# A decoder trunk on one core: weights streamed in tiles of 2048 columns instead of 1024

## The chip, the cores and the metric

The kernel runs on one NeuronCore of a Trainium2 chip. The time is the device time of one execution in microseconds (us), the median of several runs. Engines are named as in the profile: PE (TensorE, matrix products), PEld (its weight loads), DVE (VectorE), ACT (ScalarE), POOL (GpSimd) and SP (SyncE, which only issues transfers here; SPq is its queue).

## The reference, cut to what matters

512 tokens of width 1024 pass two layers. Each layer is a mixer (layer 0: pooling and retention; layer 1: HGRN2), then PEER, a layer of 16384 experts of which each token picks 8 heads x 16; all in f32:

```python
def layer(h):
    mix = mixer(h)                              # projections of h, a recurrence, a projection out
    h = layer_norm(DN_ALPHA * h + mix)
    return layer_norm(DN_ALPHA * h + peer(h))

def peer(xt, w_q, sub_keys, u_tab, v_tab):      # 128 tokens at a time
    q = (xt @ w_q).reshape(T, 8, 2, 128)
    s = einsum('thpd,hpkd->thpk', q, sub_keys)
    s_top, i_top = top_k(s, 16)                 # per half of the key
    cand = s_top[:, :, 0, :, None] + s_top[:, :, 1, None, :]
    best, pos = top_k(cand.reshape(T, 8, 256), 16)
    eid  = the 16 expert numbers of each head at pos
    gate = softmax(best)
    act  = gelu(einsum('td,thkd->thk', xt, u_tab[eid]))
    return einsum('thk,thkd->td', gate * act, v_tab[eid])
```

## The kernel before

Every weight comes from HBM in f32, and PE multiplies in a shorter format. So each weight tile is split: `stream` takes a tile of 128 x 1024 from HBM (one transfer of 512 KB on SP's queue), ACT casts it to `hi` (L75) and DVE subtracts, `lo` = raw - hi (L76). Activations are split in the same way (`xThi`, `xTlo`). A product is three matmuls, hi x hi, hi x lo, lo x hi (`mm3`, L91 to L93). The tiles lie in rotating buffers: `raw` has 5 slots, `hi` and `lo` 6 each. A slot of `raw` is free when its `lo` is done, one of `hi` or `lo` when PE has read it last.

**Projections.** A weight matrix is handled in chunks of 512 columns, each of four tiles (two slices of 128 input channels in each). For each of the four blocks of 128 tokens PE makes 24 matmuls for a chunk: 8 slices by 3. After a mixer or a PEER the new activations are normalized, transposed on PE (L158) into PSUM tiles `pC`, of which there are three, and copied out by ACT (xThi, L163) and DVE (xTlo, L164).

**PEER.** Tokens 0 to 383 are computed densely: for each of 128 blocks of 128 experts, gelu(x u) is multiplied by a table of gates that is zero where a token did not choose an expert. The gate tables `gt` are built on PE from one-hot vectors (L785, L786), written to DRAM (`gd`) and loaded back by groups of four blocks, 768 KB each (L895). While DVE and ACT find the experts, `lookahead` computes gelu(x u) of the first 14 groups (`ge`). The last 128 tokens (`gather_rounds`) gather the rows of u and v of their own experts by indirect transfers that POOL issues (L838), into six row buffers; DVE multiplies (L848) and adds (L857) them.

**The expert loop** (L861 on) goes over the blocks: multiply `ge` by `gt` (L911), split the product into `ch` (ACT) and `cl` (DVE), stream the v tile (L915), and add hi x ch, lo x ch and hi x cl to the accumulators (`mm2`, L941; 18 matmuls of 512 columns for a block). From group 14 on `front` also streams u tiles and computes gelu(x u). A round of gathers is issued when a counter asks for it. The last four blocks are kept (`TAIL`) and finished one accumulator after another.

A scheduler in the tile framework fixes the order of the instructions on each engine when the kernel is built; an engine works strictly in that order, and an instruction that waits holds up all behind it.

## Time and profile before

| | us |
|---|---|
| median of 3 runs | 2877.6 (2876.41 to 2877.6) |
| the profiled execution | 2878.49 |
| its span, first to last instruction | 2876.7 |
| PE busy | 2859.1 (99%) |
| DVE busy | 2370.6 (82%) |
| ACT busy | 1144.2 (40%) |

The profile is of one execution. A row of a timeline has start and duration in us, then engine, line, operation, what is written<-what is read, shapes, and how many in a row; in brackets the idle time before it and what ended that. PE ran at the higher of its two clock levels all the time (mean granted clock 0.999).

### The profile page before, as it was taken

Reading aid. Unit: us, or ns where it says so; the run is one execution under the profiler, and the core shown is the slowest. Engines: PE = TensorE matmul, PEld = TensorE weight load, DVE = VectorE, ACT = ScalarE, POOL = GpSimd, SP = SyncE. Lnnn points to the kernel's source line nnn. Section 1 sums busy time; section 2 is a strip of 40 time slices with the busy share of each in tenths; the row PEclk is TensorE's granted clock in tenths of the full one; section 3 lists DMA queues with packets and bytes.
Section 4 is the critical chain, followed back from the end, with each engine's and each line's share of the span. In section 5 each row is a group of like instructions: output and inputs, shape, how many; then the busy total and the mean of one; then the engine's idle time right before and its main releaser. Section 6 shows DMA issues by size and latency. Waiting matters only on the chain.

```text
span 2876.7 us, 42571 instructions
## 1 busy us (share of the span) xinstructions
PE 2859.1 (99%) x15832; PEld 2556.6 (89%) x15832; DVE 2370.6 (82%) x4482; ACT 1144.2 (40%) x1707; POOL 721.3 (25%) x539
## 2 busy tenths in 40 slices
PE   9999999999999999999999999999999999999998
PEld 7888999988898888888888889999988989889887
DVE  6779999788878888886798679999788887888786
ACT  3333565433333333333334323565433333333332
POOL 0000000045445455440000000000245454544440
PEclk9999999999999999999999999999999999999999
DMA  6223469999999999995322234479999999989982
GB/s 223 94 94 111 147 208 289 273 366 376 350 339 370 341 376 334 351 359 169 107 81 70 96 96 134 152 244 291 313 375 343 353 370 336 375 332 352 352 323 74
DMA packets 283792, 743.41 MB, mean 258 GB/s; under 512 B 21696, under 2 KB 120512, under 8 KB 283584
## 3 DMA queue, kind: packets, MB, share of 16 engines
q1 hardware_dynamic: 209856, 472.22, 47.2%
q0 software_dynamic: 73728, 268.47, 24.1%
q8 instruction: 124, 2.03, 0.3%
q14 instruction: 84, 0.69, 0.1%
HBM read 669.31 MB, written 71.30 MB: 257 GB/s over the span
## 4 chain that ended last, share of the span: by engine, by line
PE 92%; DVE 5%; DMA 1%; ACT 1%; issue 1%; POOL 0%; SPq 0%; DVEq 0%; ACTq 0%
PE pB L941 18%; PE pC L941 18%; PE pA L91 14%; PE pA L93 14%; PE pA L92 14%; PE pC L91 2%; PE pC L93 2%; PE pC L92 2%; PE pB L785 1%; PE pB L786 1%; DVE lo L76 1%; DMA row<-in_u,eid 1%; DVE oh L778 1%; DVE og L779 1%; DVE s L701 1%
## 5 line engine op out<-in xcount | busy, mean ns | idle before, releaser
L75 ACT CAST hi<-raw 128x1024 fp32r<-128x1024 f32 (+1 forms) x609 | 638.1, 1051 | 662.1 <-PE pA L92 402.2
L76 DVE TENSOR_TENSOR lo<-raw,hi 128x1024 fp32r<-128x1024 f32 (+1 forms) x609 | 737.0, 1216 | 179.0 <-ACT hi L75 170.5
L838 POOL DMA_INDIRECT row<-in_u,eid x256 | 385.6, 1506 | 1493.7 <-DMA raw<-in_peer_v 884.7
L91 PE MATMUL pA<-xThi,hi 128*128 128x384 f32 (+2 forms) x2032 | 701.2, 345 | 3.7 <-ACT xThi L163 2.7
L93 PE MATMUL pA<-xThi,lo 128*128 128x384 f32 (+2 forms) x2032 | 699.3, 344 | 0.0
L92 PE MATMUL pA<-xTlo,hi 128*128 128x384 f32 (+2 forms) x2032 | 696.8, 343 | 0.6 <-DVE xTlo L76 0.6
L91 PEld LDWEIGHTS pA<-xThi,hi 128*128 128x128 f32 x2032 | 381.9, 188 | 21.5 <-ACT xThi L163 3.1
L92 PEld LDWEIGHTS pA<-xTlo,hi 128*128 128x128 f32 x2032 | 381.8, 188 | 17.8 <-DVE xTlo L76 1.3
L93 PEld LDWEIGHTS pA<-xThi,lo 128*128 128x128 f32 x2032 | 381.6, 188 | 14.4
L75 ACT CAST ch<-ge 128x384 fp32r<-128x384 f32 x256 | 131.4, 515 | 602.5 <-PE pC L941 473.3
L838 POOL DMA_INDIRECT row<-in_v,eid x256 | 328.7, 1284 | 158.4 <-DVE h L857 100.3
L857 DVE SCALAR_TENSOR_TENSOR h<-row,cf,h 128x1024 f32<-128x1024 f32 x256 | 327.8, 1280 | 1.1 <-DMA row<-in_v,eid 0.9
L848 DVE CUSTOM_DVE_ANT_0 row<-row,x 128x1024 f32<-128x1024 f32 x256 | 311.0, 1216 | 3.5 <-DMA row<-in_u,eid 3.5
L941 PE MATMUL pB<-hi,cl 128*128 128x512 f32 x768 | 299.4, 390 | 0.3 <-DVE cl L76 0.2
L941 PE MATMUL pC<-hi,ch 128*128 128x512 f32 x768 | 299.7, 390 | 0.0
L941 PE MATMUL pB<-lo,ch 128*128 128x512 f32 x768 | 299.6, 390 | 0.0
L941 PE MATMUL pC<-hi,cl 128*128 128x512 f32 x768 | 299.3, 390 | 0.0
L941 PE MATMUL pB<-hi,ch 128*128 128x512 f32 x768 | 298.8, 389 | 0.0
L941 PE MATMUL pC<-lo,ch 128*128 128x512 f32 x768 | 298.6, 389 | 0.0
L911 DVE TENSOR_TENSOR ge<-ge,gt 128x384 f32<-128x384 f32 x256 | 134.7, 552 | 160.4 <-DMA ge<-sp 144.6
L76 DVE TENSOR_TENSOR cl<-ge,ch 128x384 fp32r<-128x384 f32 x256 | 141.1, 552 | 62.0 <-ACT ch L75 61.4
L941 PEld LDWEIGHTS pB<-hi,cl 128*128 128x128 f32 x768 | 144.1, 188 | 32.5 <-DVE cl L76 1.3
(261 smaller groups left out, 4127.6 us busy)
## 6 DMA issues: line engine op xcount, KB each, us to landing
raw<-in_peer_ut SPq DMA_DIRECT2D x256, 512.0 KB
raw<-in_peer_v SPq DMA_DIRECT2D x256, 512.0 KB
gd<-gbuf SPq DMA_DIRECT2D x24, 2048.0 KB
gt<-gd SPq DMA_DIRECT2D x64, 768.0 KB
sp<-ge SPq DMA_DIRECT2D x24, 768.0 KB
ge<-sp SPq DMA_DIRECT2D x24, 768.0 KB
raw<-in_peer_w_q SPq DMA_DIRECT2D x32, 512.0 KB
raw<-in_c_w_in SPq DMA_DIRECT2D x32, 512.0 KB
```

Of the source, the lines that this page charges most:

```text
L75: self.nc.scalar.copy(hi, src)
L76: return self.nc.vector.tensor_tensor(lo, src, hi.bitcast(F32), ALU.subtract)
L91: nc.tensor.matmul(ps, ah, bh, start=(first and i == 0), stop=False)
L92: nc.tensor.matmul(ps, ah, bl, start=False, stop=False)
L93: nc.tensor.matmul(ps, al, bh, start=False, stop=(last and i == n - 1))
L701: nc.vector.match_replace(out=s2, in_to_replace=mx[:, 0:8], in_values=sc, imm_value=NEG)
L778: nc.vector.tensor_tensor(oh, iot[:, None, None].broadcast_to(b5), per(0), ALU.is_equal)
L838: nc.gpsimd.indirect_dma_start(out=t, out_offset=None, in_=io[name], in_offset=bass.IndirectOffsetOnAxis(ap=self.eid[:, j:j + 1], axis=0))
L848: nc.vector.tensor_tensor_reduce(ur, ur, x3, 1.0, 0.0, ALU.mult, ALU.add, av[:, k:k + 1])
L857: nc.vector.scalar_tensor_tensor(acc, vr, coefs[i // GQ][:, i % GQ:i % GQ + 1], acc, ALU.mult, ALU.add)
L911: nc.vector.tensor_tensor(gv, gv, gt[:, :, b, :], ALU.mult)
L941: nc.tensor.matmul(acc[hf], a[:, ts], b[:, hf * 512:(hf + 1) * 512], start=first and i == 0, stop=last and i == 2)
```

## The change

Tiles become 128 x 2048 (8 KB in each partition). One transfer of 1 MB, one cast and one subtraction now serve half a chunk of a projection, or two expert blocks. There are 3 slots each of `raw`, `hi` and `lo` instead of 5, 6 and 6. In the expert loop the multiplication by the gates and the split into `ch` and `cl` are also done for two blocks at once (128 x 768), and the rounds of gathers are issued per two blocks. Two small buffers share room with others to make space (`sg`, `sgc`). At the start of the kernel the transposed input and the first weights are loaded in parts of 1, 1, 2, 2 and 2 slices. The host lays the weights out accordingly. The diff, without the layouts and the renamings:

```diff
 NLA = 14
 KEEP = 2
 ROT = 3
-RAW = 5
+RAW = 3
+WIDE = 2048
 QS = 8
 Y2 = 1.4
 YC = (0.0, 0.0, 1.0, 4.0)
...
         E = ctx.enter_context
         self.const = E(tc.tile_pool(name="const", bufs=1))
         self.big = E(tc.tile_pool(name="big", bufs=1))
-        self.st = E(tc.tile_pool(name="st", bufs=6))
+        self.st = E(tc.tile_pool(name="st", bufs=3))
         self.raw = E(tc.tile_pool(name="raw", bufs=RAW))
         self.sm = E(tc.tile_pool(name="sm", bufs=4))
         self.dram = E(tc.tile_pool(name="dram", bufs=1, space=DRAM))
...
         self.nc.scalar.copy(hi, src)
         return self.nc.vector.tensor_tensor(lo, src, hi.bitcast(F32), ALU.subtract)
 
+    def wide(self):
+        return (self.raw.tile([P, WIDE], F32, name="raw", tag="raw"),
+                self.st.tile([P, WIDE], F32R, name="hi", tag="hi"),
+                self.st.tile([P, WIDE], F32R, name="lo", tag="lo"))
+
     def stream(self, src):
-        nc = self.nc
-        raw = self.raw.tile([P, 1024], F32, name="raw", tag="raw")
-        nc.sync.dma_start(out=raw, in_=src)
-        hi = self.st.tile([P, 1024], F32R, name="hi", tag="hi")
-        lo = self.st.tile([P, 1024], F32R, name="lo", tag="lo")
+        raw, hi, lo = self.wide()
+        self.nc.sync.dma_start(out=raw, in_=src)
         self.split(raw, hi, lo)
         return hi, lo
 
...
                 self.layernorm(tb, hs[tb], g, b, nxT, None if layer == 0 else out)
         return nxT
 
-    def mm1(self, layer, blk, xT, dst, alt=False):
-        nc = self.nc
-        uh, ul = self.stream(self.io["peer_ut"][layer, blk])
+    def mm1(self, u, b, xT, dst, alt=False):
         if alt:
             ps = self.psC.tile([P, 512], F32, name="pC", tag="pC")
         else:
             ps = self.psA.tile([P, 512], F32, name="pA", tag="pA")
-        self.mm3(ps[:, :TD], [((uh[:, dc * P:(dc + 1) * P], ul[:, dc * P:(dc + 1) * P]),
-                               (xT[0][:, dc, :TD], xT[1][:, dc, :TD])) for dc in range(NDC)])
-        nc.scalar.activation(dst, ps[:, :TD], AF.Gelu)
+        c = [slice((b * NDC + dc) * P, (b * NDC + dc + 1) * P) for dc in range(NDC)]
+        self.mm3(ps[:, :TD], [((u[0][:, c[dc]], u[1][:, c[dc]]), (xT[0][:, dc, :TD], xT[1][:, dc, :TD]))
+                              for dc in range(NDC)])
+        self.nc.scalar.activation(dst, ps[:, :TD], AF.Gelu)
 
     def lookahead(self, layer, xT, sp):
         for g in range(NLA):
             ge = self.pe.tile([P, NB, TD], F32, name="ge", tag="ge", bufs=3)
             for b in range(NB):
-                self.mm1(layer, g * NB + b, xT, ge[:, b, :], b % 2 == 1)
+                if b % 2 == 0:
+                    u = self.stream(self.io["peer_ut"][layer, (g * NB + b) // 2])
+                self.mm1(u, b % 2, xT, ge[:, b, :], b % 2 == 1)
                 if g >= NLA - KEEP:
                     self.kept[g] = ge
                 elif b == NB - 1:
...
                     nc.sync.dma_start(out=gt, in_=gd[g])
                     ges[g] = (ge, gt)
                 if g >= NLA:
-                    self.mm1(layer, g * NB + b, xT, ges[g][0][:, b, :])
-
-            for i in range(AHEAD):
+                    u = self.stream(io["peer_ut"][layer, (g * NB + b) // 2])
+                    for k in range(2):
+                        self.mm1(u, k, xT, ges[g][0][:, b + k, :])
+
+            for i in range(0, AHEAD, 2):
                 front(i)
-            cs, vs = [], []
-            for i in range(NE):
-                if i % 2 == 0:
-                    front(i + AHEAD)
-                    front(i + AHEAD + 1)
+            tail = []
+            for i in range(0, NE, 2):
+                front(i + AHEAD)
                 g, b = order[i // NB], i % NB
                 ge, gt = ges[g]
-                gf = ge[:, b, :]
-                gv = gf.rearrange("p (s t) -> p s t", t=32)
-                nc.vector.tensor_tensor(gv, gv, gt[:, :, b, :], ALU.mult)
-                ch = ex.tile([P, TD], F32R, name="ch", tag="ch", bufs=4)
-                cl = ex.tile([P, TD], F32R, name="cl", tag="cl", bufs=4)
+                gf = ge[:, b:b + 2, :]
+                gv = gf.rearrange("p b (s t) -> p b s t", t=32)
+                nc.vector.tensor_tensor(gv, gv, gt[:, :, b:b + 2, :].rearrange("p s b t -> p b s t"), ALU.mult)
+                ch = ex.tile([P, 2, TD], F32R, name="ch", tag="ch")
+                cl = ex.tile([P, 2, TD], F32R, name="cl", tag="cl")
                 mark = self.split(gf, ch, cl)
-                v = self.stream(io["peer_v"][layer, g * NB + b])
-                cs.append((ch, cl))
-                vs.append(v)
-                if i < NE - TAIL and i % 2:
-                    for k in (i - 1, i):
+                v = self.stream(io["peer_v"][layer, (g * NB + b) // 2])
+                for k in range(2):
+                    c = (ch[:, k], cl[:, k])
+                    vk = [x[:, k * D:(k + 1) * D] for x in v]
+                    if i < NE - TAIL:
                         for tb in range(3):
-                            self.mm2(accs[tb], tb, cs[k], vs[k], k == 0, False)
-                used += 1.0 if g < NLA else 2.0
+                            self.mm2(accs[tb], tb, c, vk, i + k == 0, False)
+                    else:
+                        tail.append((c, vk))
+                used += 2.0 if g < NLA else 4.0
                 while done < (P + 8) * used / (total * 0.96):
                     done += 1
                     with tc.issue_after(mark.ins):
...
             for tb in range(3):
                 for hf in range(2):
                     for b in range(TAIL):
-                        self.mm2(accs[tb], tb, cs[b - TAIL], vs[b - TAIL], False, b == TAIL - 1, (hf,))
+                        self.mm2(accs[tb], tb, *tail[b], False, b == TAIL - 1, (hf,))
                     z = hs[tb][:, hf * 512:(hf + 1) * 512]
                     nc.vector.scalar_tensor_tensor(z, z, ALPHA, accs[tb][hf], ALU.mult, ALU.add)
 
...
     def run(self, out):
         nc, io = self.nc, self.io
         self.epst = self.const.tile([P, 1], F32, name="epst", tag="epst")
-        self.const.tile([P, 344], F32, name="gap", tag="gap")
+        self.const.tile([P, 88], F32, name="gap", tag="gap")
         nc.vector.memset(self.epst, EPS)
         hs = [self.big.tile([P, D], F32, name="h%d" % tb, tag="h%d" % tb) for tb in range(NTB)]
         xT = self.new_xT()
         self.warm()
-        w0 = []
-        for k in range(4):
-            raw = self.raw.tile([P, 2, T], F32, name="raw", tag="raw")
-            if k == 0:
-                wr = self.raw.tile([P, 2, T], F32, name="raw", tag="raw")
-                hi = self.st.tile([P, 2, T], F32R, name="hi", tag="hi")
-                lo = self.st.tile([P, 2, T], F32R, name="lo", tag="lo")
-                wsrc = io["ab_w_in"][0, 0].rearrange("p (a n) -> p a n", a=2)
-                for a in range(2):
-                    nc.sync.dma_start(out=raw[:, a], in_=io["xT"][:, a, :])
-                    nc.sync.dma_start(out=wr[:, a], in_=wsrc[:, a])
-                for a in range(2):
-                    self.split(raw[:, a], xT[0][:, a, :], xT[1][:, a, :])
-                    self.split(wr[:, a], hi[:, a], lo[:, a])
-                flat = "p a n -> p (a n)"
-                w0.append((hi.rearrange(flat), lo.rearrange(flat)))
-                continue
-            ks = slice(2 * k, 2 * k + 2)
-            nc.sync.dma_start(out=raw, in_=io["xT"][:, ks, :])
-            self.split(raw, xT[0][:, ks, :], xT[1][:, ks, :])
-            w0.append(self.stream(io["ab_w_in"][0, k]))
+        self.w0 = []
+        for k, parts in ((0, ((0, 1), (1, 2), (2, 4))), (1, ((0, 2), (2, 4)))):
+            raw = self.raw.tile([P, 4, T], F32, name="raw", tag="raw")
+            wr, hi, lo = self.wide()
+            for a, b in parts:
+                nc.sync.dma_start(out=raw[:, a:b], in_=io["xT"][:, 4 * k + a:4 * k + b, :])
+                nc.sync.dma_start(out=wr[:, a * T:b * T], in_=io["ab_w_in"][0, k][:, a * T:b * T])
+            for a, b in parts:
+                d = slice(4 * k + a, 4 * k + b)
+                self.split(raw[:, a:b], xT[0][:, d], xT[1][:, d])
+                self.split(wr[:, a * T:b * T], hi[:, a * T:b * T], lo[:, a * T:b * T])
+            self.w0.append((hi, lo))
         self.ident = self.cload("ident", [P, P])
-        self.w0 = w0
         for layer in range(2):
             self.mixer(layer, xT, hs)
             xT = self.peer(layer, hs, out)
```

Three lines are added at the head of the file, so the lines after are a few higher: the cast is L76, the subtraction L77, `mm3` L94 to L96, the transposes L161, xThi L166, xTlo L167, the gates' multiplication L915, the u rows L852.

Where the order of instructions changes. The first place is the start of PEER in layer 0, on DVE. `h2` and `h3` are residuals of token blocks 2 and 3, the other names are as above; the number behind a name marks the single tile. Before the change:

```order
L171 RECIPROCAL rs_1355<-sd_1353 128x1
L76 TENSOR_TENSOR lo_1442<-raw_1439,hi_1441 128x1024
L194 SCALAR_TENSOR_TENSOR h2_86<-h2_86,rs_1355,lnb_1289 128x512 x2
L204 SCALAR_TENSOR_TENSOR h3_87<-h3_87,pA_1254 128x512
L76 TENSOR_TENSOR lo_1448<-raw_1445,hi_1447 128x1024
L164 TENSOR_TENSOR xTlo_1293<-pC_1306,xThi_1292 128x4x128
L164 TENSOR_TENSOR xTlo_1293<-pC_1314,xThi_1292 128x4x128
L164 TENSOR_TENSOR xTlo_1293<-pC_1333,xThi_1292 128x4x128
L164 TENSOR_TENSOR xTlo_1293<-pC_1341,xThi_1292 128x4x128
L186 BN_STATS bst_1375<-h3_87 128x6
L164 TENSOR_TENSOR xTlo_1293<-pC_1360,xThi_1292 128x4x128
L164 TENSOR_TENSOR xTlo_1293<-pC_1368,xThi_1292 128x4x128
```

The same piece after the change (L77 for L76, L167 for L164):

```order
L197 SCALAR_TENSOR_TENSOR h2_86<-h2_86,rs_1287,lnb_1221 128x512 x2
L77 TENSOR_TENSOR lo_1367<-raw_1365,hi_1366 128x2048
L207 SCALAR_TENSOR_TENSOR h3_87<-h3_87,pA_1186 128x512
L77 TENSOR_TENSOR lo_1703<-raw_1701,hi_1702 128x2048
L167 TENSOR_TENSOR xTlo_1225<-pC_1238,xThi_1224 128x4x128
L167 TENSOR_TENSOR xTlo_1225<-pC_1246,xThi_1224 128x4x128
L167 TENSOR_TENSOR xTlo_1225<-pC_1265,xThi_1224 128x4x128
L167 TENSOR_TENSOR xTlo_1225<-pC_1273,xThi_1224 128x4x128
L167 TENSOR_TENSOR xTlo_1225<-pC_1292,xThi_1224 128x4x128
L167 TENSOR_TENSOR xTlo_1225<-pC_1300,xThi_1224 128x4x128
```


The two narrow `lo` ahead of the first xTlo are two wide ones now, so twice as many columns are subtracted ahead of it; before, the next narrow ones came behind the sixth xTlo.

On ACT at the same place (sd is a standard deviation), before the change:

```order
L169 ACTIVATE sd_1326<-mv_1324,epst_81 128x1
L75 CAST hi_1441<-raw_1439 128x1024
L169 ACTIVATE sd_1353<-mv_1351,epst_81 128x1
L75 CAST hi_1447<-raw_1445 128x1024
L75 CAST hi_1783<-raw_1781 128x1024
L75 CAST hi_1789<-raw_1787 128x1024
L163 CAST xThi_1292<-pC_1306 128x4x128
L163 CAST xThi_1292<-pC_1314 128x4x128
L163 CAST xThi_1292<-pC_1333 128x4x128
L163 CAST xThi_1292<-pC_1341 128x4x128
```

After the change:

```order
L172 ACTIVATE sd_1285<-mv_1283,epst_81 128x1
L76 CAST hi_1366<-raw_1365 128x2048
L76 CAST hi_1702<-raw_1701 128x2048
L166 CAST xThi_1224<-pC_1238 128x4x128
L166 CAST xThi_1224<-pC_1246 128x4x128
L166 CAST xThi_1224<-pC_1265 128x4x128
```


Four narrow casts between the standard deviations and xThi have become two wide ones. hi_1360 and hi_1366 are the first two tiles of w_q, hi_1702 the third; with three slots hi_1366 takes the one of the first half of the last chunk of the mixer's output projection, and hi_1702 the one of its second half.

The second place is the passage from layer 0 to layer 1, on ACT. Before the change:

```order
L169 ACTIVATE sd_12997<-mv_12995,epst_81 128x1
L169 ACTIVATE sd_13024<-mv_13022,epst_81 128x1
L75 CAST hi_13119<-raw_13117 128x1024
L75 CAST hi_13125<-raw_13123 128x1024
L75 CAST hi_13235<-raw_13233 128x1024
L163 CAST xThi_12963<-pC_12977 128x4x128
L163 CAST xThi_12963<-pC_12985 128x4x128
L163 CAST xThi_12963<-pC_13004 128x4x128
L75 CAST hi_13241<-raw_13239 128x1024
L163 CAST xThi_12963<-pC_13012 128x4x128
```

After the change:

```order
L172 ACTIVATE sd_11793<-mv_11791,epst_81 128x1
L172 ACTIVATE sd_11820<-mv_11818,epst_81 128x1
L76 CAST hi_11908<-raw_11907 128x2048
L76 CAST hi_12018<-raw_12017 128x2048
L166 CAST xThi_11759<-pC_11773 128x4x128
L166 CAST xThi_11759<-pC_11781 128x4x128
L166 CAST xThi_11759<-pC_11800 128x4x128
```


Three narrow casts ahead of xThi are two wide ones, and the narrow one between the copies is gone. On DVE one wide `lo` (lo_11909) stands where one narrow one stood, ahead of the first xTlo.

The third place is the start of the expert loop in layer 0, on DVE. ge_5997 (before) and ge_5713 (after) are the group that is multiplied first, gt_5998 and gt_5714 its gate table; ge_5405 and ge_5145 the second group with the second table, gt_6128 and gt_5832. Before the change:

```order
L911 TENSOR_TENSOR ge_5997<-ge_5997,gt_5998 128x384 x2
L76 TENSOR_TENSOR lo_6275<-raw_6272,hi_6274 128x1024
L76 TENSOR_TENSOR cl_6132<-ge_5997,ch_6131 128x384
L848 ISA row_6142,av_6141<-row_6142,x3_1287 128x1024
L848 ISA av_6141 128x1
L848 ISA row_6145,av_6141<-row_6145,x3_1287 128x1024
L848 ISA av_6141 128x1
L76 TENSOR_TENSOR cl_6150<-ge_5997,ch_6149 128x384
L848 ISA row_6195,av_6141<-row_6195,x3_1287 128x1024
L848 ISA av_6141 128x1
L911 TENSOR_TENSOR ge_5997<-ge_5997,gt_5998 128x384 x2
L911 TENSOR_TENSOR ge_5405<-ge_5405,gt_6128 128x384
```

After the change:

```order
L915 TENSOR_TENSOR ge_5713<-ge_5713,gt_5714 128x768
L915 TENSOR_TENSOR ge_5145<-ge_5145,gt_5832 128x768
L77 TENSOR_TENSOR cl_5836<-ge_5713,ch_5835 128x768
L852 ISA row_5882,av_5881<-row_5882,x3_1219 128x1024
L852 ISA av_5881 128x1
L852 ISA row_5885,av_5881<-row_5885,x3_1219 128x1024
L852 ISA av_5881 128x1
L852 ISA row_5888,av_5881<-row_5888,x3_1219 128x1024
L852 ISA av_5881 128x1
L915 TENSOR_TENSOR ge_5713<-ge_5713,gt_5714 128x768
L77 TENSOR_TENSOR lo_5956<-raw_5954,hi_5955 128x2048
L77 TENSOR_TENSOR cl_5893<-ge_5713,ch_5892 128x768
```


Before, the first two `cl` and three rows of gathered tokens stood ahead of the multiplication by the second table (gt_6128); now the multiplication by the second table (gt_5832) is the second instruction of the piece, ahead of the first `cl`. In layer 1 the order is the same, with other numbers.

## Rows read from the trace of the kernel before

**Rows 1.** The page, part 1: busy us (share of the span) x instructions.

```profile
PE 2859.1 (99%) x15832; PEld 2556.6 (89%) x15832; DVE 2370.6 (82%) x4482; ACT 1144.2 (40%) x1707; POOL 721.3 (25%) x539
```

**Rows 2.** PE's waits: what waited <- for what: us in total, times, longest.

```profile
PE pA L91 <- ACT xThi L163: 2.9, 3, 1.3
...
PE pA L91 <- ACT hi L75: 1.0, 1, 1.0
```

**Rows 3.** ACT's groups by shape: count | busy, mean ns | idle before, releaser.

```profile
L75 ACT CAST hi<-raw 128x1024 fp32r<-128x1024 f32 x607 | 636.8, 1053 | 660.5 <-PE pA L92 402.2 <-issue 100.3 <-PE pC L92 78.2
L75 ACT CAST ch<-ge 128x384 fp32r<-128x384 f32 x256 | 131.4, 515 | 602.5 <-PE pC L941 473.3 <-DVE ge L911 102.9 <-issue 21.2
...
L75 ACT CAST hi<-raw 128x512 fp32r<-128x512 f32 x2 | 1.2, 618 | 1.6 <-DMA raw<-in_ab_w_in 1.6
```

**Rows 4.** DVE's groups by shape.

```profile
L76 DVE TENSOR_TENSOR lo<-raw,hi 128x1024 fp32r<-128x1024 f32 x607 | 735.6, 1218 | 177.9 <-ACT hi L75 169.5 <-PE pB L786 5.4
...
L76 DVE TENSOR_TENSOR cl<-ge,ch 128x384 fp32r<-128x384 f32 x256 | 141.1, 552 | 62.0 <-ACT ch L75 61.4
...
L76 DVE TENSOR_TENSOR lo<-raw,hi 128x512 fp32r<-128x512 f32 x2 | 1.4, 688 | 1.0 <-ACT hi L75 1.0
```

**Rows 5.** Line L75: ACT's idle time ahead of it (us, times) until this.

```profile
  DMA raw<-in_peer_ut: 18.4, 5
```

**Rows 6.** Timeline of the start of PEER in layer 0.

```profile
162.78 1.47 PE L158 MATMUL pC<-c_ident,h 128*128 128x128 f32 x12
...
163.68 1.22 DVE L76 TENSOR_TENSOR lo<-raw,hi 128x1024 fp32r<-128x1024 f32 x1
163.97 1.55 ACT L163 CAST xThi<-pC 128x512 fp32r<-128x512 f32 x3
164.81 1.88 DVE L164 TENSOR_TENSOR xTlo<-pC,xThi 128x512 fp32r<-128x512 f32 x3
...
165.58 0.39 PE L91 MATMUL pA<-xThi,hi 128*128 128x256 f32 x1 [1.33 <-ACT xThi L163]
...
167.39 0.36 PE L92 MATMUL pA<-xTlo,hi 128*128 128x256 f32 x1
```

**Rows 7.** The layer boundary: first a piece of the chain of waits, then timeline.

```profile
1366.75 2.72 PE pB L941 x12
...
1381.07 2.95 ACT L75 CAST hi<-raw 128x1024 fp32r<-128x1024 f32 x3 [1.19 <-PE pC L941]
...
1383.92 1.59 ACT L163 CAST xThi<-pC 128x512 fp32r<-128x512 f32 x3
...
1384.64 0.48 PE L91 MATMUL pA<-hi,xThi 128*128 128x512 f32 x1
```

**Rows 8.** The experts' start in layer 0: timeline; then transfers from 567 to 577.

```profile
566.54 0.80 SPq L895 DMA_DIRECT2D gt<-gd  x2
...
573.27 1.03 DVE L911 TENSOR_TENSOR ge<-ge,gt 128x384 f32<-128x384 f32 x2 [4.51 <-DMA gt<-gd]
...
574.74 0.39 PE L941 MATMUL pB<-hi,ch 128*128 128x512 f32 x1
...
575.35 0.55 DVE L76 TENSOR_TENSOR cl<-ge,ch 128x384 fp32r<-128x384 f32 x1
...
581.48 1.49 DVE L911 TENSOR_TENSOR ge<-ge,gt 128x384 f32<-128x384 f32 x3
...
DMA packets 872, 3.71 MB, mean 371 GB/s; under 512 B 95, under 2 KB 95, under 8 KB 872
...
q1 hardware_dynamic: 572, 2.59, 69.9%
```

**Rows 9.** Timeline of the experts' start in layer 1.

```profile
2058.16 1.03 DVE L911 TENSOR_TENSOR ge<-ge,gt 128x384 f32<-128x384 f32 x2 [4.18 <-DMA gt<-gd]
...
2059.96 0.39 PE L941 MATMUL pB<-hi,ch 128*128 128x512 f32 x1
```

**Rows 10.** The page, part 5: the rows of u on DVE.

```profile
L848 DVE CUSTOM_DVE_ANT_0 row<-row,x 128x1024 f32<-128x1024 f32 x256 | 311.0, 1216 | 3.5 <-DMA row<-in_u,eid 3.5
```

More of the change, by code (lines that the diff above doesn't have):

```diff
@@ L98, in wchunk @@
             return w
-        return [self.stream(src[j, k]) for k in range(4)]
+        return [self.stream(src[j, k]) for k in range(2)]
     def proj_T(self, src, j, xT, sink, early=False):
@@ L224, in mixer_ab @@
             sums = self.pool_part(ab, xT, ya, w, icnt, pw, psc)
-            self.w0 = [self.stream(w[1, k]) for k in range(4)]
+            self.w0 = [self.stream(w[1, k]) for k in range(2)]
             nc.sync.dma_start(out=ng, in_=io["ret_norm_g"][0][None, :].broadcast_to([P, 512]))
```

18 lines of the change are left out of this document (9 added, 9 removed).

## The prediction

> **What bounds the kernel now.** I read the busy shares first: TensorE works 2859.1 of 2876.7 us [rows 1], so nearly all of the time is its own work. The question is then what TensorE waits for. The view of its waits answers [rows 2]: the longest entry is 2.9 us for xThi, the high half of the transposed activations, and it waited for a weight tile's high half once, 1.0 us. All entries of that view add up to about 7 us. The other engines' busy time is therefore cover, not path: the change can give back at most these 7 us, while every place where a bigger step makes TensorE wait is paid in full, because nothing later has room to make it up. The profiled execution took 2878.5 us, 0.9 above the median of 2877.6; the sum is made on it, and the median taken by adding the same difference.
>
> TensorE's matmuls themselves don't change: the same products, shapes and nearly the same order. So the work is to find the places where a tile's own chain (transfer, cast on ScalarE, subtraction on VectorE) now finishes later than TensorE asks for it.
>
> **What a wide step costs.** A cast of 1024 columns takes 1.053 us and one of 512 takes 0.618 [rows 3]: 0.435 per 512 columns, so 2048 columns take 1.053 + 2 x 0.435 = 1.92 us (estimate). A subtraction takes 1.218 at 1024 and 0.688 at 512 [rows 4]: 1.218 + 2 x 0.530 = 2.28 us (estimate). The same slope puts a `cl` over two blocks (768 columns) at 0.552 + 0.40 = 0.95 us, the multiplication at the same (two narrow ones took 1.03 [rows 8]), and a `ch` at 0.515 + 0.33 = 0.84. Per pair of blocks VectorE saves about 0.15 us each on `lo`, `cl` and `ge`, and ScalarE 0.19 on the cast. Over some 300 pairs of tiles and 128 pairs of expert blocks this is over 80 us of VectorE's time, and I count it at nothing: among TensorE's waits the one for `hi` is 1.0 us [rows 2] and those for any low half are shorter. If that cover were gone the saving could be at most the 7 us above. What grows is the latency: from a free slot to a usable `lo` was 1.05 + 1.22 = 2.3 us, and is 4.2 us.
>
> What the transfers are worth can be bounded as well. ScalarE waited for a raw transfer of `peer_ut` 18.4 us in 5 places of the whole run [rows 5], TensorE not once. The Trainium skill (DMA: Bandwidth & Descriptors, "Rules for kernel authors") asks for 1 MiB per transfer for the most bandwidth, which speaks for this change; here the trace sets the worth of that against TensorE's waits and leaves next to nothing. Its best result is the rival "faster" below.
>
> **Start of PEER (both layers), +1.9 us each.** The last chunk of the mixer's output projection ends at 162.78 [rows 6]. Before, ScalarE casts two more w_q tiles and starts xThi at 163.97; TensorE waits 1.33 us for it. With three wide slots the second wide tile of the next chunk (hi_1366) takes the slot of the old chunk's first tile, free 12 matmuls before the end (12 take 2.72 [rows 7]), about 160.1; it is done by 162.1. The tile after it (hi_1702) needs the slot that is free at 162.8, runs 163.0 to 164.9, and stands ahead of xThi in ScalarE's row. xThi starts 0.95 late. On VectorE the two wide subtractions stand ahead of the first xTlo: lo_1367 162.15 to 164.4, the residual addition to 165.0, lo_1703 to about 167.3. Before, the second `lo` started at 163.68 and the first xTlo at 164.81 [rows 6]. The transposes that follow reuse the PSUM tile that each xTlo has read; the sixth waits for the third xTlo, which was done at 166.69 (164.81 + 1.88) and now is at 167.3 + 1.9 = 169.2. TensorE's first L92 then comes at about 169.3 instead of 167.39: +1.9. In layer 1 the same rows stand 1485 us later, so +3.8 in all. The bounds: +0.95 per layer, if only the cast matters, and +2.5, if the wide operations run 10% over the estimate: 1.9 to 5.
>
> **Layer boundary, +1.5 us.** The experts' last six groups of 12 matmuls begin at 1366.75 and end near 1382.9 [rows 7]; TensorE goes on with the next mixer's first L91 at 1384.64. The tail holds two tiles to its end. Before, three short casts ran from 1381.07 and xThi followed at 1383.92. Now hi_11908 gets the slot of the tail's first pair about 6 matmuls (1.4 us) before the end, 1381.6 to 1383.5, and hi_12018 that of the second pair, to 1385.4; xThi is behind both: 1385.4 against 1383.92, +1.5. VectorE's lo_11909 (to about 1386.5) delays xTlo by 1.3, which is no more. Bounds 0.9 to 2.
>
> **Start of the experts (both layers), +6.6 us.** This is the largest term. The two gate tables `gt` of the first two groups are requested at 566.54; the first lets VectorE multiply at 573.27 after 4.51 us of waiting; `cl` follows at 575.35 [rows 8]. The second table was wanted only by the third multiplication of the group that starts at 581.48. Now VectorE's row has the multiplication by the **second** table directly behind the first, ahead of the first `cl`. So `cl`, the rows of the gathered tokens and everything behind wait for the second load. When does it land? After 573.27 and before 582.42 (581.48 + two thirds of 1.49) by the rows. Between: the queue of these loads moved 69.9% of 371 GB/s there, 259 GB/s [rows 8]; 0.79 MB more takes 3.0 us, and 5.1 us if the 0.52 MB weight tile requested behind it gets its share at once. I take the middle, 577.3. Then the multiplication 0.95 and `cl` 0.95 end at 579.2, where TensorE, without waiting, would ask at 574.74 + 4 x 0.23 = 575.65: **3.5 us**. In layer 1 the first table is there at 2058.16 and the first matmul comes later, at 2059.96 [rows 9]: the second at 2062.1 by the same rates, `cl` at 2064.0, asked for at 2060.9: **3.1 us**. Nothing gives that back: the next pair's `cl` comes behind three rows of 1.3 us, another multiplication and a wide `lo`, about 8 us after the first, which is what 36 matmuls last (8.2 us), so the delay is passed on and not repeated. Bounds per layer: 0.4 us (the table lands with the first; only the wider `ch` counts) and 8.7 us (582.42 + 1.9 - 575.65): 0.8 to 17.4.
>
> **Everywhere else, 0.** *Inside the expert loop* TensorE reads a pair for 8.2 us (36 matmuls of 0.227) or more, against a chain of 4.2 us, and had no wait there. *Chunk changes:* the second wide tile of the next chunk has the window from 12 matmuls before the end of the old chunk to 12 after: 24 x 0.227 = 5.45 us for 4.2 us of work. It fits with 1.2 us to spare, and that is the rival below. *Start:* the first parts of xT and weights are as large as before; the later ones are together as large. 0, or up to 1 us late. *Gathers:* VectorE waited 3.5 us in all for u rows [rows 10]; issued in bursts of three rounds at most, they keep the same six buffers.
>
> **Sum.** 3.8 + 1.5 + 6.6 = 11.9 us: 2890.4 beside the profiled 2878.5, and from the median **2889.5 us**. The bounds of the three terms add up to 3.6 and 24.4, which gives 2881 to 2902 from the median.
>
> **The rivals.** *Same, about 2882 (chance 0.21):* the second gate table is there when the first is, since both are requested in one go and share 16 engines; then the experts' start costs 0.8, and with PEER's start at its lower bound of 1.9 and the boundary's 1.5 the sum is +4.2. For it: VectorE's wait of 4.51 us was ended by the first table alone, and no row shows the second's end. Against it: the queue's rate, by which the second needs at least 3 us more. The point is 575.3: a table that is usable by then costs little. *Faster, about 2871 (0.06):* the larger transfers and the fewer fixed parts remove the waits of 7 us and the three terms don't appear, because VectorE, relieved of 0.15 us per operation, reaches them earlier. Against it: freed slots and the landed table, not the engines, set the times there. *Much slower, about 2909 (0.11):* the chunk changes. There are some 20 of them in the projections; the window leaves 1.2 us, so one further operation of 0.7 us ahead of the wide tile fits in, two do not. If each is missed by 1 us, 20 are added to the 11.9. For it: VectorE is busy for most of the span [rows 1] and also does the lookup there; against it: in most chunk changes the wide cast stands ahead of the last copies out of PSUM in ScalarE's row. *The forecast* (0.62) is the rest.
>
> **How the numbers follow.** A measurement of this kernel tells about 0.2% (5.8 us) from no change: 2871.8 to 2883.4. Faster has the chance of its rival, 0.06. Same takes the rival of 0.21 and 0.04 of the forecast's low end: 0.25. Slower is the rest, 0.69. The range leaves out the faster rival and the much slower one (0.17 together). It goes from 2877, no change at all, since the bounds of the same case lie between that and 2884, to 2902, the upper bound of the sum.
>
> **What the profile after would show.** Right: TensorE waits for `cl` some 3 us once per layer at the experts' start, with VectorE's second multiplication waiting for gt<-gd just before; first low-half matmul of PEER about 6.5 us after the transposes begin, not 4.6; first matmul of the second mixer 3 us after the experts' end, not 1.7; TensorE's waits near 19 us in all. Wrong: a wait for `hi` or `lo` at many chunk changes (the slower rival), no wait for `cl` (the same), or VectorE waiting for u or v rows many times, which none of my terms holds. If the wide cast takes other than 1.9 us or the wide subtraction other than 2.3, the first two terms are wrong in size.

## The result, and the profile after

The changed kernel takes **2892.8 us** (median of 5 runs, 2889.0 to 2896.1) against 2877.6 (5 runs): ratio 1.0052, 95% interval 1.0038 to 1.0067. It is slower by 15 us, three from the forecast of 2889.5. The two times agree better than their parts do: the largest term never appeared, another was nearly twice as large, places held at nothing cost 9 us, and a gain was overlooked.

The page after, parts 1 and 5 (compare [rows 1], [rows 3], [rows 4]):

```profile
PE 2862.6 (99%) x15832; PEld 2558.5 (89%) x15832; DVE 2337.3 (81%) x3924; ACT 1086.3 (38%) x1277; POOL 844.0 (29%) x539
...
L77 DVE TENSOR_TENSOR lo<-raw,hi 128x2048 fp32r<-128x2048 f32 (+1 forms) x307 | 694.8, 2263 | 176.8 <-ACT hi L76 176.6
L76 ACT CAST hi<-raw 128x2048 fp32r<-128x2048 f32 (+1 forms) x307 | 580.5, 1893 | 419.5 <-PE pA L95 262.3
...
L76 ACT CAST ch<-ge 128x768 fp32r<-128x768 f32 x128 | 107.0, 836 | 614.3 <-PE pC L947 601.0
...
L77 DVE TENSOR_TENSOR cl<-ge,ch 128x768 fp32r<-128x768 f32 x128 | 122.3, 956 | 228.5 <-ACT ch L76 228.5
```

The wide steps cost what was estimated (the estimate in brackets): 1.89 us (1.92), 2.26 (2.28), 0.84 (0.84) and 0.96 (0.95). TensorE works 3.5 us more than before in a span that is 13.5 longer. The rest, 10 us, is idle time, and the view of TensorE's waits, which answers [rows 2], names it:

```profile
PE pA L94 <- ACT xThi L166: 6.0, 4, 2.2
PE pA L96 <- DVE lo L77: 4.0, 4, 1.7
PE pA L94 <- ACT hi L76: 3.3, 2, 2.4
PE pC L161 <- DVE xTlo L167: 1.8, 3, 0.8
...
PE pC L290 <- DVE kn L280: 0.7, 1, 0.7
...
```

The whole view has no wait for `cl`. There are new ones for `lo` and `kn`.

To see where the time went I matched TensorE's matmuls of each kernel with the same matmuls before, in order, and read how much later each begins; the steps of that lag belong to places. Worked out from the timelines of the profiled runs, in us:

| place | forecast | after | e1_order | e3_halves | e9_halves_mended |
|---|---|---|---|---|---|
| start | 0 | +2.3 | +2.2 | +3.0 | +0.2 |
| retention | 0 | +1.3 | +1.3 | +0.6 | 0 |
| PEER's start, layer 0 | +1.9 | +3.4 | +0.1 | +0.1 | 0 |
| lookup, layer 0 | 0 | +2.8 | +3.8 | +1.3 | +1.3 |
| gates and experts' start, layer 0 | +3.5 | -1.8 | -2.2 | -2.4 | -3.0 |
| boundary | +1.5 | +2.1 | 0 | 0 | 0 |
| PEER's start, layer 1 | +1.9 | +3.4 | 0 | 0 | 0 |
| lookup, layer 1 | 0 | +2.6 | +2.7 | +1.3 | +1.2 |
| gates and experts' start, layer 1 | +3.1 | -2.0 | -2.0 | -2.6 | -2.6 |
| end | +11.9 | +14.1 | +6.0 | +1.4 | -2.8 |

The last row is the lag of the last matmul. Inside the expert loops and at the chunk changes of the projections the lag stays level.

### The profile page after: what moved, and what is told of

The parts are those of the page before. It is cut to its first block, busy times and chain, and to the rows that moved or that the text cites. A ratio compares the mean times of both kernels' runs of the same rounds, so it can differ in the third digit from the quotient of the medians.

```text
span 2890.2 us, 40151 instructions
## 1 busy us (share of the span) xinstructions
PE 2862.6 (99%) x15832; PEld 2558.5 (89%) x15832; DVE 2337.3 (81%) x3924; ACT 1086.3 (38%) x1277; POOL 844.0 (29%) x539
## 4 chain that ended last, share of the span: by engine, by line
PE 87%; DVE 11%; DMA 1%; ACT 1%; issue 1%; POOL 0%; SPq 0%; DVEq 0%; ACTq 0%; POOLq 0%
PE pC L947 17%; PE pB L947 17%; PE pA L96 13%; PE pA L94 13%; PE pA L95 13%; DVE lo L77 2%; PE pB L789 2%; PE pB L790 1%; PE pC L94 1%; PE pC L96 1%; PE pC L95 1%; DVE s L705 1%; DVE ix L707 1%; DVE ix L704 1%; ACT hi L76 1%
## 5 line engine op out<-in xcount | busy, mean ns | idle before, releaser
L842 POOL DMA_INDIRECT row<-in_u,eid x256 | 483.2, 1888 | 1404.6 <-issue 927.8
L77 DVE TENSOR_TENSOR lo<-raw,hi 128x2048 fp32r<-128x2048 f32 (+1 forms) x307 | 694.8, 2263 | 176.8 <-ACT hi L76 176.6
L76 ACT CAST hi<-raw 128x2048 fp32r<-128x2048 f32 (+1 forms) x307 | 580.5, 1893 | 419.5 <-PE pA L95 262.3
L94 PE MATMUL pA<-xThi,hi 128*128 128x384 f32 (+2 forms) x2032 | 700.9, 345 | 7.6 <-ACT xThi L166 4.4
L96 PE MATMUL pA<-xThi,lo 128*128 128x384 f32 (+2 forms) x2032 | 699.2, 344 | 4.0 <-DVE lo L77 4.0
L94 PEld LDWEIGHTS pA<-xThi,hi 128*128 128x128 f32 x2032 | 381.9, 188 | 25.5 <-ACT xThi L166 4.8
L96 PEld LDWEIGHTS pA<-xThi,lo 128*128 128x128 f32 x2032 | 382.2, 188 | 19.5 <-DVE lo L77 5.3
L842 POOL DMA_INDIRECT row<-in_v,eid x256 | 353.9, 1382 | 132.5 <-DVE h L861 66.2
L76 ACT CAST ch<-ge 128x768 fp32r<-128x768 f32 x128 | 107.0, 836 | 614.3 <-PE pC L947 601.0
L852 DVE CUSTOM_DVE_ANT_0 row<-row,x 128x1024 f32<-128x1024 f32 x256 | 312.1, 1222 | 1.1 <-DMA row<-in_u,eid 1.1
L77 DVE TENSOR_TENSOR cl<-ge,ch 128x768 fp32r<-128x768 f32 x128 | 122.3, 956 | 228.5 <-ACT ch L76 228.5
L653 ACT ACTIVATE ge<-pA 128x384 f32<-128x384 f32 x200 | 97.8, 489 | 226.7 <-PE pA L96 226.6
```

The costliest lines, as they stand in the source:

```text
L76: self.nc.scalar.copy(hi, src)
L77: return self.nc.vector.tensor_tensor(lo, src, hi.bitcast(F32), ALU.subtract)
L94: nc.tensor.matmul(ps, ah, bh, start=(first and i == 0), stop=False)
L96: nc.tensor.matmul(ps, al, bh, start=False, stop=(last and i == n - 1))
L653: self.nc.scalar.activation(dst, ps[:, :TD], AF.Gelu)
L842: nc.gpsimd.indirect_dma_start(out=t, out_offset=None, in_=io[name], in_offset=bass.IndirectOffsetOnAxis(ap=self.eid[:, j:j + 1], axis=0))
```

## The experiments

Numbers without an interval come from one profiled run each. Runs of the changed kernel alone lie 7 us apart, so such a run is judged by its places more than by its total.

**PEER's start and the boundary: is it the row order?** The theory says that a wide cast and subtraction stand ahead of the activations' copies. The edit puts the third wide tile's steps of the next chunk behind the sixth of those copies (`pinned` is 3 at PEER's start and the boundary), and leaves slots and transfers alone.

```diff
+        if self.nstream == self.pinned:
+            self.behind(self.last, self.copies[5])
```

> The changed kernel with one difference in order: the third wide tile of the next projection (cast and subtraction) is issued behind the sixth copy of the transposed activations, at the start of PEER in both layers and at the layer boundary. Theory (a wide step that stands ahead of the copies in the row of ScalarE and VectorE costs TensorE its length): the 3.4 us per layer at PEER's start and the 1.8 us at the boundary come back, some 8.5 us in all, span near 2882; TensorE's first low-half matmul of PEER about 4.5 us after the transposes begin. Rival (three slots are too few, whatever the order): the tile that is cast later is missing when its chunk begins, TensorE waits for hi or lo there instead, and the span stays within 2 us of 2890.

Measured: 2883.9 us, span 2882.1 against 2890.2. The losses at PEER's start and at the boundary are gone, +3.4 to +0.1, +2.1 to 0, and +3.4 to 0; one more is paid at the lookup of layer 0, where the clock fell to 0.50 (338 to 340) behind a wait of 1.76 us; behind the same wait of 1.70 the changed kernel kept 1.00. Here is PEER's start after, first ScalarE and VectorE, then TensorE, and the same of TensorE in e1_order (timelines: start, us, engine, line, operation, idle before and what ended it):

```profile
166.72 1.91 ACT L76 CAST hi<-raw 128x2048 fp32r<-128x2048 f32 x1 [0.81 <-PE pA L96]
168.53 1.55 ACT L166 CAST xThi<-pC 128x512 fp32r<-128x512 f32 x3
...
168.76 2.29 DVE L77 TENSOR_TENSOR lo<-raw,hi 128x2048 fp32r<-128x2048 f32 x1
170.96 1.88 DVE L167 TENSOR_TENSOR xTlo<-pC,xThi 128x512 fp32r<-128x512 f32 x3
...
166.48 1.47 PE L161 MATMUL pC<-c_ident,h 128*128 128x128 f32 x12
170.14 0.51 PE L94 MATMUL pA<-xThi,hi 128*128 128x256 f32 x2 [2.19 <-ACT xThi L166]
...
171.70 2.82 PE L161 MATMUL pC<-c_ident,h 128*128 128x128 f32 x12 [0.82 <-DVE xTlo L167]
174.17 0.56 PE L95 MATMUL pA<-xTlo,hi 128*128 128x256 f32 x1
```

```profile
166.34 1.47 PE L172 MATMUL pC<-c_ident,h 128*128 128x128 f32 x12
168.64 0.38 PE L105 MATMUL pA<-xThi,hi 128*128 128x256 f32 x1 [0.83 <-ACT xThi L177]
...
169.35 1.85 PE L172 MATMUL pC<-c_ident,h 128*128 128x128 f32 x12
170.96 0.36 PE L106 MATMUL pA<-xTlo,hi 128*128 128x256 f32 x1
```

From the first transposes to the first low-half matmul: 7.7 us after, 4.6 in e1_order, 4.61 before [rows 6]. The theory holds. But the second twelve transposes took 2.82 us after and 1.85 in e1_order, and no wait is in that. The columns of TensorE by stretch show why: us, PE busy (matmuls), granted clock, DMA share, GB/s. After:

```profile
168.00:170.00 2.00, 0.00 (x0) 1.00 0.41 70
170.00:172.00 2.00, 1.04 (x6) 0.83 0.85 352
172.00:174.00 2.00, 2.00 (x11) 0.50 1.02 377
174.00:176.00 2.00, 2.00 (x16) 0.81 0.59 250
```

and e1_order:

```profile
170.00:172.00 2.00, 2.00 (x18) 1.00 0.94 389
```

After its idle 2.2 us and the short work with another 0.8 us of waiting, TensorE ran at 0.50, the lower of its two levels (1.2 GHz), between 172 and 174 and for a part of the stretches on either side (0.83 and 0.81). In e1_order it idled 0.83 us and stayed at 1.00. So a part of the loss is the wait, and a part is slower matmuls behind it.

**Is it the length of the step or the number of slots?** The rival to step length: three slots of 2048 are coarser than six of 1024, and so late slots, not long steps, cost the time. Here slots and 1 MB transfers stay, and each tile is cast and subtracted in two halves.

```diff
-        self.split(raw, hi, lo)
+        for i in range(2):
+            c = slice(i * 1024, (i + 1) * 1024)
+            self.split(raw[:, c], hi[:, c], lo[:, c])
```

> The changed kernel with the same slots and the same 1 MB transfers, but each tile is cast and subtracted in two steps of 1024 columns (the start, the ch and cl of two blocks stay as they are). Theory (what costs is the length of one step in a row, and that TensorE must wait for the whole of it): most of the loss at PEER's start (3.4 to 4.2 us per layer), at the boundary (1.8) and in the lookup (2.4 and 2.6) comes back, span near 2880, and TensorE's clock stays at its upper level there. Rival (three slots, each freed late, cost, whatever the length of a step): losses at these places stay within 1 us of the changed kernel's, span 2888 to 2892.

Measured: 2879.3 us, span 2877.5. Both starts of PEER and the boundary are at zero with the slots unchanged, retention and lookup are about halved. So three slots don't cost that time by themselves; the long steps do. PEER's start in e3_halves:

```profile
166.61 1.05 ACT L76 CAST hi<-raw 128x1024 fp32r<-128x1024 f32 x1 [0.72 <-ACT hi L76]
167.27 1.22 DVE L77 TENSOR_TENSOR lo<-raw,hi 128x1024 fp32r<-128x1024 f32 x1
168.40 1.88 DVE L169 TENSOR_TENSOR xTlo<-pC,xThi 128x512 fp32r<-128x512 f32 x3
169.00 1.07 ACT L76 CAST hi<-raw 128x1024 fp32r<-128x1024 f32 x1
...
170.98 0.36 PE L97 MATMUL pA<-xTlo,hi 128*128 128x256 f32 x1
```

One half of the third tile still stands ahead of the copies, the other goes behind the first three. The shorter step and the new order come together here; e1_order shows the order alone. The loss at the kernel's start remains.

**The start of the kernel.** Parts of xT are staged in raw slots there, and the second half of the first weights is requested only at 12.77 us. The edit stages xT in the residual tiles, which are empty then.

```diff
-            raw = self.raw.tile([P, 4, T], F32, name="raw", tag="raw")
...
-                nc.sync.dma_start(out=raw[:, a:b], in_=io["xT"][:, 4 * k + a:4 * k + b, :])
+                for d in range(a, b):
+                    nc.sync.dma_start(out=hs[2 * k + d // 2][:, d % 2 * T:(d % 2 + 1) * T], in_=io["xT"][:, 4 * k + d, :])
```

> The changed kernel, but at the start the transposed input is loaded into the residual buffers, which are idle then, so that the three raw slots hold weights alone. Theory (the later half of the first chunk waited for a raw slot that held the input, issued at 12.8 us): its transfers are issued in the first 5 us, TensorE's loss of 2.3 us in the first 18 us is gone, span near 2888. Rival (the start is bound by the bytes that arrive, not by the slots): the transfers compete earlier, the gain is under 0.5 us or the first matmul comes later.

Measured: the start's loss goes from 2.3 to 0.1 us, and yet the kernel takes 2892.4, because PEER's start in layer 0 cost 4.2 instead of 3.4 and the boundary 3.3 instead of 2.1. The code is the same at these places; the clock is not. TensorE by stretch at the boundary, first after, then e2_start (its waits there, 1.41 and 0.24 us, are as long as after's):

```profile
1394.00:1396.00 2.00, 1.56 (x5) 1.00 0.00 0
1396.00:1398.00 2.00, 2.00 (x16) 1.00 0.90 246
```

```profile
1394.00:1396.00 2.00, 2.00 (x9) 0.50 0.48 143
1396.00:1398.00 2.00, 2.00 (x12) 0.79 0.90 381
```

The same happens at the kernel's start. Its wait is for the second slice of weights, first after, then before:

```profile
9.02 0.62 ACT L76 CAST hi<-raw 128x512 fp32r<-128x512 f32 x1 [2.51 <-DMA raw<-in_ab_w_in]
9.69 0.50 PE L94 MATMUL pA<-xThi,hi 128*128 128x512 f32 x1 [2.38 <-ACT hi L76]
```

```profile
8.38 0.62 ACT L75 CAST hi<-raw 128x512 fp32r<-128x512 f32 x1 [1.61 <-DMA raw<-in_ab_w_in]
9.05 0.50 PE L91 MATMUL pA<-xThi,hi 128*128 128x512 f32 x1 [1.00 <-ACT hi L75]
```

TensorE is 0.6 us late there. No wait follows in the first 20 us, so the request at 12.77, which the theory blames, costs nothing; the remaining 1.6 of the 2.3 are matmuls at a clock of 0.73 and 0.50 between 10 and 14 us. With the same code and 1.00 there (e5_twice, e6_pin) the loss is 0.9. With this edit it is 0.1 and 0.2 at 1.00 (e2_start, e9_halves_mended) and 1.5 at 0.50 (e8_best). So the edit is worth about 0.8 us and the clock 1.4, and a single total could not have told them apart. Why the second slice lands earlier with the edit (cast at 8.48) was not isolated.

**The experts' start.** The forecast's largest term was that the first `cl` stands behind the second gate table. After, there is no such wait. These are SP's requests and VectorE's row of layer 0 after:

```profile
572.51 0.80 SPq L899 DMA_DIRECT2D gt<-gd  x2
579.07 0.33 SPq L86 DMA_DIRECT2D raw<-in_peer_ut  x1
...
579.14 0.96 DVE L915 TENSOR_TENSOR ge<-ge,gt 128x768 f32<-128x768 f32 x1
581.95 0.96 DVE L915 TENSOR_TENSOR ge<-ge,gt 128x768 f32<-128x768 f32 x1 [1.85 <-DMA gt<-gd]
582.82 0.95 DVE L77 TENSOR_TENSOR cl<-ge,ch 128x768 fp32r<-128x768 f32 x1
...
584.03 0.40 PE L947 MATMUL pB<-hi,cl 128*128 128x512 f32 x1
```

VectorE did wait for the second table (1.85 us), in the order that was foreseen, and `cl` was done at 583.7, 0.3 before TensorE wanted it. To see that the chain exists and only its price was missing, one kernel loads the second table twice and keeps the first `cl` behind its multiplication; another takes the second table's multiplications out of `cl`'s way.

```diff
+                    if g == order[1]:
+                        nc.sync.dma_start(out=gt, in_=gd[g])
```

> The changed kernel, but the second gate table is loaded twice in a row into the same buffer at the start of the expert loop, and the first cl stays queued behind the multiplication by it. Theory (the mechanism of the forecast holds, and only its price vanished because the table landed in time): the second copy lands some 7 us later, TensorE waits 6 to 8 us for cl in each layer, span near 2904. Rival (VectorE's row has enough lead there to absorb a late table): under 2 us in all.

```diff
+                if i in (4, 6):
+                    tc.add_manual_dep(m.ins, marks[0].name, ...)
```

> The changed kernel, but the multiplications by the second gate table are queued behind the first cl. Theory (the table was there in time, so its place in the row costs nothing): no change, within 0.7 us of 2890. Rival (the forecast's step: the first cl is held up by that multiplication, and TensorE with it): 3 us gained in each layer, span near 2884.

Measured: e5_twice takes 2909.0 us; it loses 7.8 and 8.8 us at the two places, and these are its waits (behind them the clock fell to 0.50, for instance from 590 to 594):

```profile
PE pB L953 <- DVE cl L77: 13.3, 2, 6.8
```

e6_pin takes 2892.8 (span 2891.0, just outside the 0.7 us that were allowed), no gain: it waits 1.2 us in two places for a later `cl`. The chain is real, its price in the changed kernel is zero.

**The two-block `ch`/`cl` alone.** The kernel before with only the multiplication and split of two blocks at once; tiles of 1024 and six slots stay.

```diff
+                    ch2 = ex.tile([P, 2, TD], F32R, name="ch", tag="ch")
+                    cl2 = ex.tile([P, 2, TD], F32R, name="cl", tag="cl")
+                    mark = self.split(gf, ch2, cl2)
+                ch, cl = ch2[:, i % 2], cl2[:, i % 2]
```

> The kernel before, with only the multiplication by the gates and the split into ch and cl done for two blocks at once. Theory (VectorE's relief in the expert loop is cover and not path): within 1 us of 2876.7, and none of the losses of the changed kernel appears; the gain of some 1.8 us per layer in the gate matmuls does not appear either, since that stage has no such steps. Rival (the larger steps of the expert loop are where the change gains or loses): 3 us or more either way.

Measured: 2880.2 us, span 2878.4, which is between theory and rival. Layer 0 gains 0.5 at the experts' start, layer 1 loses 2.9 (TensorE waits 1.6 us for `ch` and 0.8 for `cl`), so these steps are not cover alone; no gain in the gate stage. So the gain there, which the changed kernel has, doesn't come from this part.

**The lookup.** TensorE waits there 1.7 us for a `lo` whose `hi` had been ready 5 us earlier: VectorE, busy for all of the 16 us from 326 to 342, began it behind its lookup work.

```profile
328.66 3.73 ACT L76 CAST hi<-raw 128x2048 fp32r<-128x2048 f32 x2
...
337.58 2.27 DVE L77 TENSOR_TENSOR lo<-raw,hi 128x2048 fp32r<-128x2048 f32 x1
...
339.91 0.44 PE L96 MATMUL pA<-xThi,lo 128*128 128x384 f32 x1 [1.70 <-DVE lo L77]
```

The edit lets these weight tiles go ahead by about 100 instructions in the scheduler's order.

```diff
-                    u = self.stream(self.io["peer_ut"][layer, (g * NB + b) // 2])
+                    with self.tc.high_priority(offset=100):
+                        u = self.stream(self.io["peer_ut"][layer, (g * NB + b) // 2])
```

> The changed kernel, but the streamed u tiles of the lookahead are put some 100 instructions earlier in the scheduler's order of preference, so that on VectorE they stand ahead of more of the lookup. Theory (in the lookup stage VectorE has no idle time and the wide subtraction is queued too late): TensorE's waits for lo there, 4.0 us in 4 places, fall under 1 us, and the stage loses under 1 us in each layer instead of 2.4 and 2.6, span near 2886. Rival (VectorE is full there, so what is put ahead pushes something else that TensorE needs): waits move to the scores or the gates and the span stays within 2 us of 2890.

Measured: 2895.6 us. The wait for `lo` is gone and TensorE waits for the lookup's own results:

```profile
PE pC L758 <- DVE ka L831: 2.7, 2, 1.3
PE pC L758 <- DVE kb L831: 2.7, 4, 0.7
```

VectorE is full in this stage; order alone moves the wait. The lookups lose 3.5 and 3.4 us instead of 2.8 and 2.6. The rival held in its mechanism; the span of 2893.9 is above its 2 us, since the boundary cost 3.7, with the clock at the lower level there.

**Mended versions.** e8_best joins e1_order, e2_start, e7_prio and a rule that keeps two `lo` behind the retention's multiplications, with undivided wide steps.

```diff
+        if self.late is not None and self.nstream in (2, 3):
+            self.behind(self.last[1:], (self.late,))
```

> The changed kernel with all mends together: input staged outside the raw slots at the start, third wide tile behind the sixth copy at PEER's start and at the boundary, two wide subtractions behind the masked scores in the retention, and the u tiles of the lookahead preferred. Theory (the losses are separate places, and the gain of the change itself is the 4 us in the gate stage and the experts' start): losses of 2.3, 1.3, 7, 1.8 and 5 us go, about 2873 to 2875 us, that is 3 to 4 us under the kernel before. Rival (each mend moves its wait to the next place): 2878 to 2884, no faster than before.

Measured: 2882.2 us (11 runs), ratio 1.0016, interval 1.0007 to 1.0025. The expectation was missed and the rival's range holds: the lookups still cost 4.1 us (with a clock of 0.50 from 358 to 360) and 3.3, and the start 1.5 at a clock of 0.50. Since e3_halves had the better answer, the next one joins the halves with the same repairs, but without e7_prio's.

> The changed kernel with each tile cast and subtracted in two steps of 1024 columns (as in e3_halves), the input staged outside the raw slots at the start (e2_start), the third tile behind the sixth copy (e1_order) and the two subtractions behind the masked scores in the retention; the lookahead's preference of e7_prio is left out. Theory (with short steps only the start, 2.9 us, and small waits were left, and the gate stage's gain of 1.8 us per layer stays): 2873 to 2876 us, ratio to the kernel before about 0.999. Rival (the start's loss and the waits come back elsewhere): 2878 or more.

Measured: 2876.0 us (11 runs) against 2877.5 (15 runs), ratio 0.9996, interval 0.9987 to 1.0005: not to be told from the kernel before, and at the upper edge of what was expected. The -2.8 of the table compares two single profiles. Its losses are the lookups, 1.3 us each, and its gain is mainly that of the gate stage, 2.2 us in each layer.

**Does the transfer's size bring anything?** e3_halves with two transfers of 512 KB for each tile.

```diff
-        self.nc.sync.dma_start(out=raw, in_=src)
...
+            self.nc.sync.dma_start(out=raw[:, c], in_=src[:, c])
```

> e3_halves with each 1 MB transfer split into two of 512 KB into the same tile. Theory (the size of a transfer is not on the path, since TensorE waits for steps and not for bytes): within 1 us of e3_halves, 2877.5. Rival (the fewer and larger transfers are what brings the gain in the gate stage and the experts): 2 us or more slower, with the gain of 1.8 us per layer in the gate stage gone.

Measured: 2882.5 us, 3.2 more than e3_halves. By place: 0.7 at the kernel's start, where the clock was at 0.50 from 10 us on, and 1.3 and 1.2 at the experts' starts, where TensorE now waits for `cl` (2.0 us in two places). The gate stage's gain is as large as with 1 MB (2.2 us). So neither theory nor rival held whole. The Trainium skill (DMA: Bandwidth & Descriptors, "Rules for kernel authors") asks for at least 1 MiB per transfer for the most bandwidth; here that shows at most at the experts' starts, where weights, gathers and gate tables load together. One run of each can't settle 2 us.

More slots of 2048 columns, the other way to loosen the order, were not tried; two small buffers already share room to make three fit.

## Why the prediction was right in sum and wrong in its parts

**The bound and the direction: right.** The time lost is TensorE's waiting or its slower clock, nearly everywhere at places where a long step stands ahead of work that is due. That the sum came within 3 us is luck: the experts' start, +6.6 in the forecast, came to -0.9, and the gate stages gave 2.9; against that PEER's starts cost 3.0 more, the boundary 0.6 more and the places held at nothing 9.0. The waits add up to about 19 us, as forecast, but they are other waits: none of the 6.6 for `cl` is among them.

**PEER's start: right mechanism, mis-sized.** The step "TensorE's first L92 then comes at about 169.3" (6.5 us after the transposes) rested on the third xTlo being done 6.4 us after them. It was done at 170.96 + 1.88 = 172.84, 6.36 after: so far the chain was read rightly. The end of the sum was not. It puts the first L92 0.1 us behind the third xTlo; in the rows of before it stands 0.7 behind (167.39 less 166.69 [rows 6]), since transposes come between. That is 0.6 of the 1.5 missing between 1.9 and 3.4. The other 0.9 (an estimate, what is left) goes with the lower clock: the second twelve transposes took 2.82 us instead of 1.85 in e1_order, and the first two matmuls behind them 0.36 and 0.21 instead of 0.20 and 0.11. In layer 1 it is the same (the clock was 0.50 between 1664 and 1666).

**The boundary: right.** By the lag 1.4 us come at the first matmul, against 1.5, and 0.7 behind it, which the forecast held at nothing. TensorE's first matmul of the second mixer comes 3.1 us after its last transposes began:

```profile
1389.75 3.71 ACT L76 CAST hi<-raw 128x2048 fp32r<-128x2048 f32 x2 [1.60 <-PE pC L947]
...
1390.91 1.65 PE L161 MATMUL pC<-c_ident,h 128*128 128x128 f32 x12
...
1393.99 0.50 PE L94 MATMUL pA<-hi,xThi 128*128 128x512 f32 x1 [1.43 <-ACT xThi L166]
```

**The experts' start: wrong, the largest term.** The order was right (both multiplications ahead of `cl`), the step that failed is "When does it land?". It had the second table 10.8 us after its request and TensorE asking 9.1 after it. It came after 9.4 (581.95 less 572.51), and TensorE asked 11.5 after (584.03 less 572.51). Of that shift of 3.8 us (from 3.5 late to 0.3 early) 1.4 is the landing: the weight tile that was counted as competition was requested only at 579.07, when a slot came free; another of 1 MB had been requested at 570.75, 1.8 us ahead of the tables, which the forecast didn't have. The other 2.4 are the request, which came earlier against TensorE, since TensorE had fallen 8 us behind by then and the queue's work only 6. I had moved the change's order into the times of the kernel before, at a place where a change upstream moves the two sides differently. What part either tile has in the 1.4 was not isolated by a run.

**"Everywhere else, 0": wrong in three places.** *Start*, 2.3 us: "0, or up to 1 us late" held only where the clock stayed up (0.9 in e6_pin); the other 1.4 go with the clock. *Retention*, 1.3 us: a `lo` of 2.29 us (from 78.80) stands ahead of the multiplications `kn` and another (from 82.21) between these and `sc`, where a step of 1.22 stood before. *Lookup*, 2.8 and 2.6 us: I argued with VectorE's savings and with windows for chunk changes, and did not look for a stage in which VectorE is full for hundreds of small steps. The last two are the same mechanism as PEER's start, and e3_halves shows it by about halving them; the start is a slice of weights that lands later. The test that the forecast should have made is to go through each stage and ask what stands behind a `lo` on VectorE, rather than what stands behind the tile's slot.

**The gain that was not seen: 1.4 and 1.5 us in the gate stages** (the rest of those rows of the table, 0.4 and 0.5, comes at the first uses of `cl` at the experts' starts). TensorE there alternates gate matmuls (L785 before, L789 after) with the lookahead's projections. Before, the sum of every block is cut after two matmuls:

```profile
484.62 0.42 PE L91 MATMUL pA<-xThi,hi 128*128 128x384 f32 x1
484.88 0.34 PE L92 MATMUL pA<-xTlo,hi 128*128 128x384 f32 x1
485.26 0.22 PE L785 MATMUL pB<-og,oh 128*128 128x128 f16 x1
```

After, the cuts stand elsewhere, such as this one:

```profile
500.60 0.34 PE L95 MATMUL pC<-xTlo,hi 128*128 128x384 f32 x1
500.77 0.23 PE L789 MATMUL pB<-og,oh 128*128 128x128 f16 x1
```

From the last projection matmul to the gate's first it is 0.38 us there and 0.17 here. In 130 us of layer 0's stage, 16 of 39 such steps cost 0.37 or 0.38 before, and 9 of 40 cost 0.34 or 0.35 after: 16 x 0.20 less 9 x 0.17 is 1.7 us, somewhat more than the lag shows (1.4). e4_pairs, with the tiles of before, has the 39 steps at the same mean as before (0.26) and no gain; e3_halves has 31 steps there, 9 of them at 0.37 or 0.38, and gains 2.2. So the place is known: where the order of the matmuls cuts the sums. In before and e3_halves the costly cuts come after two matmuls, in the changed kernel after seven. Why some cuts cost 0.2 us more was not tested.

**The rivals.** *Much slower* fell: no chunk change waits. *Same* was right that the table costs nothing, though not in its premise (the second table came later than the first, and VectorE waited 1.85 us for it), and its total fell, since other losses took the table's place. *Faster* fell: what the larger transfers are worth on TensorE's path is at most the 2.5 us of e10_half_dma at the experts' starts, and it did not outweigh the losses.

## What to carry to other kernels

A merged step saves busy time but lengthens the longest piece of work that can stand ahead of something urgent; on an engine that feeds a busy TensorE, look in every stage for what is queued behind one such step, not only for whether the step itself is in time. Merging the transfer while keeping the steps short (e3_halves, e9_halves_mended) avoided most of the loss here. A sum that comes out right is no proof of its terms: compare the two traces place by place.

## What the runs showed of the hardware

TensorE's waits can cost more than their length. After 2.2 us of idling and a little work the granted clock fell to 0.50 (1.2 GHz) at PEER's start, and 12 transposes took 2.82 us in place of 1.85; at the boundary the wait of 1.43 us was followed by stretches at 1.00, but with the same wait in e2_start it fell to 0.50. In the lookup of layer 0 a wait of 1.70 us was followed by 1.00 in the changed kernel, and one of 1.76 by 0.50 in e1_order. That goes with runs of the changed kernel lying 7 us apart and those of the kernel before 3. The Trainium skill (TensorE: Matmul & The Clock Gate, "Part 1: The HAM clock gate") says that the level follows the engine's recent activity and that its timing varies from run to run; these rows agree.
